# Relu and square of a finished block issued behind the next product's splits, and the two-block group put first in the first down step

## The chip, the cores and the metric

The kernel runs on one core of one Trainium2 chip. The metric is device time in microseconds (us) of one execution, and the time quoted is the median over runs.

## The reference, cut to what matters

One decoder layer: a normalised input feeds three head groups (stick-breaking attention, an SSD scan, an HGRN2 scan), their outputs are projected back, and then comes the squared-ReLU MLP. The change lies wholly in that MLP.

```python
hn = rmsnorm(h, norm_mlp_w[l])
h = h + jnp.square(jax.nn.relu(hn @ w_up[l])) @ w_down[l]
return h[:, CHUNK:]
```

After the meta tokens are dropped there are 1024 tokens; w_up is 1024 x 4096 and w_down 4096 x 1024, all float32.

## The kernel before, in words

**Products.** Both MLP products are done by a Strassen-like scheme: seven products of sums of half-size blocks instead of eight of blocks. A float32 operand is split into a rounded high part and a remainder (`split`, line 1138: ScalarE casts the high part, VectorE subtracts it from the source), and a product is taken as high x high, high x low and low x high. So a product of the up projection (`product`, line 1175) is 12 matmuls of 128 x 512: four blocks of the contraction times three.

**Up projection.** w_up is taken in 16 groups q of two column blocks. Two of the seven products of each q (names L) run first. The other five form a *quad* and run in the order written out in `order_` (line 1509): S5(q), R7(q), R6(q+1), S3(q), R4(q), then S5(q+1) and so on. `right_mm` (line 1280) accumulates R6, R7 and R4 of one q in one PSUM bank (tag pa, two buffers) and S5 and S3 in another (tag pc, two buffers). Behind each product but S5 stands a drain on VectorE (`right_post`, line 1288): R6's sum goes to `ra`; R7's drain is two additions, from the pa bank and then from the pc bank, and makes block u22; S3's drain makes u12, R4's makes u21. S3 accumulates in the same pc bank that R7's second addition reads, so S3's first matmul has to wait for it. Each of u22, u12 and u21 then gets Relu and Square on ScalarE (`square`, line 1257); u22 and u12 are also stored to DRAM (`dr_s[6]`, `dr_s[3]`).

**Sums of the blocks.** The next projection needs sums of the four squared blocks u22, u11, u12, u21. `u_sums(q, 0)` (line 1264) makes two on VectorE, `u_sums(q, 1)` two on GpSimd, each with a store through SyncE's queue. They are issued one and two items behind R4(q). Other work on GpSimd: four subtractions for a later q's weights (`sum_1`, `sum_2`, `sum_4`), the second of them the input of that q's R6 (`t2s`).

**Down projection.** It runs in 17 steps of seven products. `STEPS` (line 1311) lists for each step pairs (t, ks): t is one of four token blocks, ks the blocks of the contraction, 3 matmuls each. Step 0 holds t=1 with one block and t=2 with two, 9 matmuls in each product. Each (step, t) has its own accumulating bank; the first two banks of tag pa in step 0 are those that the last two quads leave. The weights of this projection are split by `t_aux` (line 1366; the hidden activations by `s_aux`, line 1387), which also makes sums (GpSimd for the first 14, VectorE after); the first `t_aux` is issued 24 items before the down projection begins, at D0.

**What sets the order.** The main loop (line 1558) goes through `order_`. For each item i it issues, in this order: the split of item i+2 (`prep`), the side jobs listed for i (`at`: loads, sums, `t_aux`, `s_aux`), the matmuls of i, and the drain of i. VectorE, ScalarE, GpSimd and SyncE work through what was issued to them strictly in that order (`Pinned`), and TensorE takes the products in the order of `order_`. Split tiles have the tag k4 and four buffers.

Of the kernel before, what the change touches and what calls it, by code (L numbers as in the profile page):

```python
# [68 lines left out]
def tile_hybrid_block(  # L69
# [34 lines left out]
    V, A, G, SY = (Pinned(e) for e in (nc.vector, nc.scalar, nc.gpsimd, nc.sync))  # L104
# [28 lines left out]
    def sb(shape, tag, dt=F32):  # L133
        if tag in ring:
            r = ring[tag]
            r[3] += 1
            at = r[0] + r[3] % r[1] * r[2]
            return cx[:, at:at + shape[0]]
        cnt[0] += 1
        return pool.tile([P] + list(shape), dt, tag=tag, bufs=BUFS[tag], name=f"{tag}_{cnt[0]}")  # L140
# [8 lines left out]
    def dram(shape, name):  # L149
        return drp.tile(list(shape), F32, name=name)  # L150
# [13 lines left out]
    dr_s = [dram([NQ, P, 512], f"dr_s{i}") for i in range(7)]  # L164
# [27 lines left out]
    def run(steps):  # L192
        for _ in steps:
            pass
# [1006 lines left out]
    def left_mm(q, h):  # L1201
        if h == 0:
            banks[q] = ps(("mf", "pb", "mf", "mq")[q % 4])
        yield from product(banks[q], lw[q, h], [hn[a][:, 4 * h:4 * h + 4] for a in range(2)], start=h == 0)

    def left_post(q, h):
        if h == 0:
            t = sb([512], ("a1", "a3")[q % 2])
            A.copy(t, banks[q])
            SY.dma_start(dr_m[q], t)  # L1210
        else:
            t = sb([512], ("a4", "sst")[q % 2])
            A.activation(t, banks[q], AF.Relu)
            A.activation(t, t, AF.Square)
            SY.dma_start(dr_s[0][q], t)
# [37 lines left out]
    def c_tile(q, i):  # L1253
        us[q, i] = sb([512], (("a4", "st", "st", "st"), ("qb", "sst", "a2", "f4"))[q % 2][i])
        return us[q, i]

    def square(c):
        A.activation(c, c, AF.Relu)
        A.activation(c, c, AF.Square)

    def u11_load(q):
        SY.dma_start(c_tile(q, 1), dr_s[0][q])
# [17 lines left out]
    def right_mm(o, q):  # L1280
        if o == "R6":
            Rb[q] = ps("pa")
        elif o == "S5":
            Sb[q] = ps("pc")
        yield from product(Sb[q] if o[0] == "S" else Rb[q], rw[o, q],
                           S[{"R6": "s2", "S5": "s1", "R7": "s3", "S3": "s4", "R4": "22"}[o]], start=o in ("R6", "S5"))

    def right_post(o, q):
        if o == "R6":
            ra[q] = sb([512], ("igt", "f4")[q % 2])  # L1290
            V.tensor_tensor(ra[q], Rb[q], m1s[q], op=ALU.add)
        elif o == "R7":
            c = c_tile(q, 0)
            V.tensor_tensor(c, Rb[q], m1s[q], op=ALU.add)
            V.tensor_tensor(c, Sb[q], c, op=ALU.add)
            square(c)
            SY.dma_start(dr_s[6][q], c)
        elif o == "S3":
            c = c_tile(q, 2)
            V.tensor_tensor(c, Sb[q], ra[q], op=ALU.add)  # L1300
            square(c)
            SY.dma_start(dr_s[3][q], c)
        elif o == "R4":
            c = c_tile(q, 3)
            V.tensor_tensor(c, Rb[q], m1s[q], op=ALU.add)
            square(c)

    STEPS = [[(1, [0]), (2, [0, 1])], [(3, [0, 1, 2])]]
    STEPS += [[(s % 4, list(range(s, s + 4)))] for s in range(13)]
    STEPS += [[(1, [13, 14, 15])], [(2, [14, 15]), (3, [15])]]
    acc, Tu, Su, Tr, Sr, slabs = {}, {}, {}, {}, {}, []
# [18 lines left out]
    def s_unit(o):  # L1333
        if o not in Su:
            if o < 4:
                t = sb([K4], "k4", F32R)[:, 0:D].rearrange("p (a k n) -> p a k n", a=2, n=P)
                Su[o] = [t[:, 0], t[:, 1]]
            else:
                Su[o] = [sb([512], t, F32R).rearrange("p (k n) -> p k n", n=P)
                         for t in (("st", "st"), ("a1", "a3"), ("a4", "st"))[o - 4]]  # L1340
        return Su[o]
# [9 lines left out]
    def s_load(m):  # L1351

        s, o = divmod(m, 7)
        if s >= len(STEPS):
            return
        Sr[m] = sb([512], ("wT", "wT", "a5", "igt")[m % 4]).rearrange("p (k n) -> p k n", n=P)
        n = 0
        for t, ks in STEPS[s]:
            src = dr_s[o][ks[0]:ks[-1] + 1, :, t * P:(t + 1) * P]
# [27 lines left out]
    def s_aux(m):  # L1387
        s, o = divmod(m, 7)
        n = sum(len(ks) for _, ks in STEPS[s])
        u = s_unit(o)  # L1390
# [24 lines left out]
    def down_mm(s, o):  # L1415
        n = 0
        for t, ks in STEPS[s]:
            c = CHAIN[o][0]
            key = (t, c) if c == "T" else (s, t, c)
            start = key not in down_banks  # L1420
            if start:
                down_banks[key] = ps({"R": "pa", "S": "pc", "T": M2B[t]}[c])
            pd = down_banks[key]
            ops = [(i, a, b) for i in range(len(ks)) for a, b in ((0, 0), (0, 1), (1, 0))]
            for m, (i, a, b) in enumerate(ops):
                mm(pd, lhsT=Su[o][a][:, n + i, :], rhs=t_unit(o, ks[i])[:, b, :], start=start and m == 0,
                   stop=m == len(ops) - 1, skip_group_check=not start)
                yield
            n += len(ks)

    def down_post(s, o):
        c, i, j = CHAIN[o]
        for t, ks in STEPS[s]:
            end = ks[-1] == NQ - 1
            if c == "T" and not end:
                continue
            r = t + 4 * i
            if r not in acc:
                acc[r] = sb([G3], "g3")[:, 0:D]
            rs, cs = place(t, i, j)  # L1440
            dst = acc[r][:, cs]
            bank = down_banks[(t, c) if c == "T" else (s, t, c)]
            if (r, j) in begun:
                V.tensor_tensor(dst, bank, dst, op=ALU.add)
            else:
                A.copy(dst, bank)
                begun.add((r, j))
            if end and o >= 3:
                SY.dma_start(outf[rs, cs], dst)
# [72 lines left out]
    def when(i, fn, *args):  # L1522
        at.setdefault(max(0, i), []).append((fn, args))

    for q in range(NQ):
        i6, i7, i4 = (order_.index((o, q)) for o in ("R6", "R7", "R4"))
        when(i6 - 8, quad_load, q)
        when(i6 - 4, sum_1, q)
        when(i6 - 3, sum_2, q)
        when(i6 - 2, m1_load, q)  # L1530
        when(i4 + 1, u_sums, q, 0)
        when(i4 + 2, u_sums, q, 1)
        when(i7, u11_load, q)
    for b in ("11", "12", "22", "21"):
        when(D0 - 28, t_load, b, 0)
# [11 lines left out]
    def prep(i):  # L1547
        if i < D0:
            it = order_[i]
            if it[0] == "L":  # L1550
                if i:
                    left_prep(it[2], it[1])
            else:
                right_prep(*it)
# [3 lines left out]
    for i, it in enumerate(order_):  # L1558
        if i + 2 < len(order_):
            prep(i + 2)  # L1560
        for fn, args in at.get(i, ()):
            fn(*args)
        if it[0] == "L":
            run(left_mm(it[2], it[1]))
            left_post(it[2], it[1])
            next(bg, None)
        elif it[0] == "D":
            run(down_mm(it[1], it[2]))
            down_post(it[1], it[2])
        else:  # L1570
            run(right_mm(*it))
            right_post(*it)
# [23 lines left out]
```

## Time and profile before

| | |
|---|---|
| median of 3 runs | 1271.08 us (1270.58 to 1273.02) |
| the profiled execution's own time | 1271.42 us |
| its span | 1269.4 us |
| TensorE matmul busy | 1215.4 us, 96% of the span |
| VectorE busy | 868.9 us, 68% |
| ScalarE busy | 582.8 us, 46% |
| GpSimd busy | 426.9 us, 34% |
| quads (R6 of q=0 to the last R4) | 719 to 951 us after the span's start |
| down projection | 951 to 1263 us |

In the views, PE is TensorE, PEld its weight loads, DVE VectorE, ACT ScalarE, POOL GpSimd and SPq the queue of SyncE that issues DMAs. A row of a timeline gives the start, the duration, engine, line and operation, out<-in (tags without buffer numbers and without digits: k is k4, a is a1 to a5), and in brackets the idle time in front of it with what ended that. Nearly everything has line 96 or 119, since two helpers record the instructions; tiles tell them apart. A matmul's row ends later than the next one starts, because matmuls are pipelined: 12 in a row start over 2.72 us.

### The profile page before, as it was taken

How to read it: one execution, taken by the hardware profiler on the slowest of the kernel's cores; microseconds unless marked ns; L12 is line 12 of the kernel's file. 1: busy time of each engine (PE TensorE's matmuls, PEld its weight loads, DVE VectorE, ACT ScalarE, POOL GpSimd, SP SyncE). 2: the span in 40 equal slices, each digit the busy share in tenths (PEclk: the TensorE clock that was granted, in tenths of full speed). 3: DMA queues.
4: the chain of work that ended last, by engine and by line, in shares of the span. 5: the costliest groups of instructions: out<-in, count | busy, mean ns of one | idle time of the engine just before them, and what ended most of it. 6: DMA issues, size and time to landing. Idle time of an engine off the chain costs nothing.

```text
span 1269.4 us, 18555 instructions
## 1 busy us (share of the span) xinstructions
PE 1215.4 (96%) x6362; PEld 1037.4 (82%) x6362; DVE 868.9 (68%) x1449; ACT 582.8 (46%) x1237; POOL 426.9 (34%) x500
## 2 busy tenths in 40 slices
PE   7999999999999889998999999999797999999998
PEld 6989899999888777777788887777576888888887
DVE  5777777774325688787356665566667787787777
ACT  6755666664322323322366544444455544344331
POOL 4223223322103476667342656566731000000000
PEclk9999999999999899999999999999998999999999
DMA  6311111242335754561256666767656645545556
GB/s 205 93 40 45 57 43 49 70 126 81 94 103 140 231 155 111 121 134 39 83 183 192 214 205 211 232 226 249 213 173 199 179 143 150 166 142 149 165 188 207
DMA packets 195031, 184.14 MB, mean 145 GB/s; under 512 B 14405, under 2 KB 149853, under 8 KB 194938
## 3 DMA queue, kind: packets, MB, share of 16 engines
q1 hardware_dynamic: 194938, 182.97, 48.2%
q8 instruction: 50, 0.82, 0.3%
q14 instruction: 43, 0.35, 0.1%
HBM read 128.25 MB, written 54.67 MB: 144 GB/s over the span
## 4 chain that ended last, share of the span: by engine, by line
PE 64%; DVE 15%; ACT 8%; issue 6%; DMA 4%; POOL 3%; SPq 0%; ACTq 0%; DVEq 0%; POOLq 0%
PE mf L119 23%; PE pa L119 17%; PE pc L119 11%; PE mq L119 7%; DVE k L96 5%; PE pb L119 3%; ACT k L96 3%; DVE g L96 2%; DVE a L96 2%; DVE qb L96 1%; ACT a L96 1%; PE pb L122 1%; POOL cx L96 1%; DVE st L96 1%; PE pa L122 1%
## 5 line engine op out<-in xcount | busy, mean ns | idle before, releaser
L119 PE MATMUL pa<-g,k 128*128 128x512 f32 x864 | 211.2, 392 | 8.3 <-DVE f L96 6.7
L119 PEld LDWEIGHTS pa<-g,k 128*128 128x128 f32 x864 | 162.4, 189 | 44.3 <-DVE f L96 7.2
L119 PE MATMUL mf<-g,wsA 128*128 128x384 f32 (+2 forms) x624 | 139.3, 358 | 0.0
L119 PE MATMUL mf<-g,wsB 128*128 128x384 f32 (+2 forms) x624 | 136.5, 355 | 0.0
L96 DVE TENSOR_TENSOR k<-g,k 128x512 fp32r<-128x512 f32 x80 | 74.9, 937 | 69.6 <-ACT k L96 69.6
L119 PEld LDWEIGHTS mf<-g,wsA 128*128 128x128 f32 x624 | 104.4, 190 | 6.5 <-DVE wsA L96 0.3
L119 PEld LDWEIGHTS mf<-g,wsB 128*128 128x128 f32 x624 | 103.6, 189 | 6.1
L119 PE MATMUL mf<-g,g 128*128 128x512 f32 (+1 forms) x408 | 100.8, 394 | 0.0
L96 ACT CAST g<-cx 128x512 fp32r<-128x512 f32 x80 | 49.6, 620 | 83.5 <-DVE cx L96 59.9
L119 PEld LDWEIGHTS mf<-g,g 128*128 128x128 f32 (+1 forms) x408 | 72.4, 183 | 15.1 <-issue 0.3
L119 PE MATMUL pc<-g,k 128*128 128x512 f32 x336 | 83.2, 391 | 0.0
L96 DVE TENSOR_TENSOR g<-pa,g 128x512 f32<-128x512 f32 (+2 forms) x82 | 54.9, 678 | 38.4 <-PE pa L119 32.2
L96 POOL TENSOR_TENSOR cx<-cx 128x384 f32<-128x384 f32 (+2 forms) x34 | 39.0, 1147 | 120.4 <-ACT cx L96 78.5
L119 PEld LDWEIGHTS pc<-g,k 128*128 128x128 f32 x336 | 63.7, 190 | 13.4
L119 PE MATMUL mf<-g,k 128*128 128x512 f32 x288 | 69.6, 392 | 1.8 <-ACT a L96 1.5
L119 PE MATMUL pa<-g,st 128*128 128x512 f32 x240 | 65.0, 389 | 0.0
L119 PEld LDWEIGHTS mf<-g,k 128*128 128x128 f32 x288 | 53.6, 188 | 13.6 <-ACT a L96 1.9
L96 POOL TENSOR_TENSOR g<-g,g 128x512 f32<-128x512 f32 x32 | 46.3, 1454 | 49.7 <-issue 45.5
L96 DVE TENSOR_TENSOR g<-cx,g 128x512 fp32r<-128x512 f32 x80 | 57.0, 712 | 7.0 <-ACT g L96 5.6
L96 ACT CAST k<-g 128x512 fp32r<-128x512 f32 x80 | 48.9, 613 | 15.6 <-PE pb L119 11.4
L96 DVE TENSOR_TENSOR k<-wT,k 128x512 fp32r<-128x512 f32 (+1 forms) x56 | 40.7, 726 | 18.7 <-ACT k L96 18.7
L119 PEld LDWEIGHTS pa<-g,st 128*128 128x128 f32 x240 | 45.0, 188 | 9.6 <-ACT g L96 0.2
(358 smaller groups left out, 2713.7 us busy)
## 6 DMA issues: line engine op xcount, KB each, us to landing
g<-in_w_up_dram SPq DMA_DIRECT2D x48, 512.0 KB, 4.8
st<-in_w_in_dram SPq DMA_DIRECT2D x51, 256.0 KB, 2.9
cx<-in_w_down_dram SPq DMA_DIRECT2D x48, 256.0 KB, 2.9
wT<-dr_s SPq DMA_DIRECT2D x45, 256.0 KB, 2.9
dr_s<-a SPq DMA_DIRECT2D x40, 256.0 KB, 2.0
g<-in_x_dram SPq DMA_DIRECT2D x16, 512.0 KB, 5.3
dr_s<-st SPq DMA_DIRECT2D x32, 256.0 KB, 2.2
a<-dr_s SPq DMA_DIRECT2D x23, 256.0 KB, 2.9
```

The lines of the kernel that those rows point to most:

```text
L96: i = fn(*a, **k)
L119: return queue(nc.tensor.matmul(*a, **k))
L122: return queue(nc.tensor.transpose(*a, **k))
```

## The change

`square` no longer follows the drain at once. `right_post` puts the finished block (and its store, if it has one) on a list `late`; the main loop takes it from there in the next item, after that item's split and side jobs and before its matmuls. The two `u_sums` of a q are issued one item later than before. In step 0 of the down projection the group t=2 with two blocks now comes before t=1 with one.

```diff
--- before.py
+++ after.py
@@ -1254,9 +1254,13 @@
         us[q, i] = sb([512], (("a4", "st", "st", "st"), ("qb", "sst", "a2", "f4"))[q % 2][i])
         return us[q, i]
 
-    def square(c):
+    late = []
+
+    def square(c, dst=None):
         A.activation(c, c, AF.Relu)
         A.activation(c, c, AF.Square)
+        if dst is not None:
+            SY.dma_start(dst, c)
 
     def u11_load(q):
         SY.dma_start(c_tile(q, 1), dr_s[0][q])
@@ -1293,22 +1297,20 @@
             c = c_tile(q, 0)
             V.tensor_tensor(c, Rb[q], m1s[q], op=ALU.add)
             V.tensor_tensor(c, Sb[q], c, op=ALU.add)
-            square(c)
-            SY.dma_start(dr_s[6][q], c)
+            late.append((c, dr_s[6][q]))
         elif o == "S3":
             c = c_tile(q, 2)
             V.tensor_tensor(c, Sb[q], ra[q], op=ALU.add)
-            square(c)
-            SY.dma_start(dr_s[3][q], c)
+            late.append((c, dr_s[3][q]))
         elif o == "R4":
             c = c_tile(q, 3)
             V.tensor_tensor(c, Rb[q], m1s[q], op=ALU.add)
-            square(c)
-
-
-
-
-    STEPS = [[(1, [0]), (2, [0, 1])], [(3, [0, 1, 2])]]
+            late.append((c,))
+
+
+
+
+    STEPS = [[(2, [0, 1]), (1, [0])], [(3, [0, 1, 2])]]
     STEPS += [[(s % 4, list(range(s, s + 4)))] for s in range(13)]
     STEPS += [[(1, [13, 14, 15])], [(2, [14, 15]), (3, [15])]]
     acc, Tu, Su, Tr, Sr, slabs = {}, {}, {}, {}, {}, []
@@ -1528,8 +1530,8 @@
         when(i6 - 4, sum_1, q)
         when(i6 - 3, sum_2, q)
         when(i6 - 2, m1_load, q)
-        when(i4 + 1, u_sums, q, 0)
-        when(i4 + 2, u_sums, q, 1)
+        when(i4 + 2, u_sums, q, 0)
+        when(i4 + 3, u_sums, q, 1)
         when(i7, u11_load, q)
     for b in ("11", "12", "22", "21"):
         when(D0 - 28, t_load, b, 0)
@@ -1560,6 +1562,8 @@
             prep(i + 2)
         for fn, args in at.get(i, ()):
             fn(*args)
+        while late:
+            square(*late.pop(0))
         if it[0] == "L":
             run(left_mm(it[2], it[1]))
             left_post(it[2], it[1])
```

On ScalarE, in a quad in the middle (that from 757 us on in the trace), there stood before, from the Square of S3's block on (k4_1083 is R7's high part, st_1087 R4's block, k4_1088 the high part for R6, k4_1091 that for S3, qb R7's block, k4_1094 that for R4):

```order
L96 ACTIVATE st_1082_7399<-st_1082_7399 128x512 x2
L96 CAST k4_1083_7404<-g3_1051_7178 128x512
L96 ACTIVATE st_1087_7426<-st_1087_7426 128x512 x2
L96 CAST k4_1088_7430<-wT_1084_7407 128x512
L96 CAST k4_1091_7453<-g3_1052_7180 128x512
L96 ACTIVATE qb_1093_7474<-qb_1093_7474 128x512 x2
L96 CAST k4_1094_7480<-g3_1052_7180 128x512
```

On ScalarE at the same place there stands now:

```order
L96 CAST k4_1083_7401<-g3_1051_7175 128x512
L96 ACTIVATE st_1082_7399<-st_1082_7399 128x512 x2
L96 CAST k4_1088_7428<-wT_1084_7404 128x512
L96 ACTIVATE st_1087_7426<-st_1087_7426 128x512 x2
L96 CAST k4_1091_7449<-g3_1052_7177 128x512
L96 CAST k4_1094_7473<-g3_1052_7177 128x512
L96 ACTIVATE qb_1093_7470<-qb_1093_7470 128x512 x2
```

Each pair of Relu and Square (`ACTIVATE ... x2`) has moved behind one cast: R7's high part no longer stands behind S3's Square, nor R6's behind R4's, nor R4's behind R7's.

On VectorE in the same quad, from the low part for R7 on (st_1087<-pa is R4's drain, the two rows with only st and a4 are `u_sums`, the two qb rows R7's drain), before:

```order
L96 TENSOR_TENSOR k4_1083_7404<-g3_1051_7178,k4_1083_7404 128x512
L96 TENSOR_TENSOR st_1087_7426<-pa_1061_7251,a1_1055_7206 128x512
L96 TENSOR_TENSOR k4_1088_7430<-wT_1084_7407,k4_1088_7430 128x512
L96 TENSOR_TENSOR a4_1076_7358<-st_1087_7426,a4_1076_7358 128x512
L96 TENSOR_TENSOR st_1087_7426<-st_1075_7344,st_1087_7426 128x512
L96 TENSOR_TENSOR k4_1091_7453<-g3_1052_7180,k4_1091_7453 128x512
L96 TENSOR_TENSOR qb_1093_7474<-pa_1078_7367,a3_1072_7322 128x512
L96 TENSOR_TENSOR qb_1093_7474<-pc_1090_7440,qb_1093_7474 128x512
L96 TENSOR_TENSOR k4_1094_7480<-g3_1052_7180,k4_1094_7480 128x512
```

On VectorE at the same place there stands now:

```order
L96 TENSOR_TENSOR k4_1083_7401<-g3_1051_7175,k4_1083_7401 128x512
L96 TENSOR_TENSOR st_1087_7426<-pa_1061_7251,a1_1055_7200 128x512
L96 TENSOR_TENSOR k4_1088_7428<-wT_1084_7404,k4_1088_7428 128x512
L96 TENSOR_TENSOR k4_1091_7449<-g3_1052_7177,k4_1091_7449 128x512
L96 TENSOR_TENSOR a4_1076_7354<-st_1087_7426,a4_1076_7354 128x512
L96 TENSOR_TENSOR st_1087_7426<-st_1075_7340,st_1087_7426 128x512
L96 TENSOR_TENSOR qb_1093_7470<-pa_1078_7367,a3_1072_7316 128x512
L96 TENSOR_TENSOR qb_1093_7470<-pc_1090_7436,qb_1093_7470 128x512
L96 TENSOR_TENSOR k4_1094_7473<-g3_1052_7177,k4_1094_7473 128x512
```

The two sums have moved behind the low part for S3 (k4_1091); they still stand ahead of R7's drain.

On VectorE where the up projection ends (st_1299<-pa is R4's drain of q=14, a2<-pc S3's of q=15, f4<-pa R4's of q=15, which is the last product; g1 rows are `t_aux`, the 128x384 rows `s_aux` of step 0), before:

```order
L96 TENSOR_TENSOR st_1299_8907<-pa_1267_8671,a1_1261_8620 128x512
L96 TENSOR_TENSOR a4_1280_8777<-st_1299_8907,a4_1280_8777 128x512
L96 TENSOR_TENSOR st_1299_8907<-st_1279_8763,st_1299_8907 128x512
L96 TENSOR_TENSOR g1_1300_8915<-kto_62,g1_1300_8915 128x512
L96 TENSOR_TENSOR k4_1301_8919<-wT_1283_8789,k4_1301_8919 128x384
L96 TENSOR_TENSOR a2_1303_8937<-pc_1292_8843,f4_1287_8811 128x512
L96 TENSOR_TENSOR g1_1300_8915<-cx_61,g1_1300_8915 128x512
L96 TENSOR_TENSOR k4_1304_8949<-a5_1284_8792,k4_1304_8949 128x384
L96 TENSOR_TENSOR f4_1306_8967<-pa_1286_8798,a3_1276_8741 128x512
L96 TENSOR_TENSOR qb_1295_8877<-f4_1306_8967,qb_1295_8877 128x512
L96 TENSOR_TENSOR f4_1306_8967<-sst_1294_8859,f4_1306_8967 128x512
```

On VectorE at the same place there stands now:

```order
L96 TENSOR_TENSOR st_1299_8907<-pa_1267_8671,a1_1261_8614 128x512
L96 TENSOR_TENSOR g1_1300_8909<-kto_62,g1_1300_8909 128x512
L96 TENSOR_TENSOR k4_1301_8913<-wT_1283_8786,k4_1301_8913 128x384
L96 TENSOR_TENSOR a2_1303_8933<-pc_1292_8843,f4_1287_8811 128x512
L96 TENSOR_TENSOR a4_1280_8773<-st_1299_8907,a4_1280_8773 128x512
L96 TENSOR_TENSOR st_1299_8907<-st_1279_8759,st_1299_8907 128x512
L96 TENSOR_TENSOR g1_1300_8909<-cx_61,g1_1300_8909 128x512
L96 TENSOR_TENSOR k4_1304_8942<-a5_1284_8789,k4_1304_8942 128x384
L96 TENSOR_TENSOR f4_1306_8963<-pa_1286_8798,a3_1276_8735 128x512
L96 TENSOR_TENSOR g1_1300_8909<-cx_61,g1_1300_8909 128x512
L96 TENSOR_TENSOR cx_61<-cx_61 128x512
```

The sums of q=14 have moved from ahead of S3's drain to behind it, and those of q=15 from right behind the last drain to behind three more operations of the down projection.

## The prediction

> **What bounds the kernel now.** I read the busy table and the page's 40 slices first (TensorE is busy 96% of the span and at full clock nearly throughout), then what TensorE waits for in the stretch that the change touches, then the timelines of TensorE, VectorE and ScalarE around the longest waits. TensorE's waits from the first quad to the second down step (microseconds in total, times, longest):
>
> ```profile
> PE pa L119 <- DVE f L96: 6.7, 1, 6.7
> PE pc L119 <- DVE qb L96: 4.0, 4, 2.5
> PE pc L119 <- DVE a L96: 3.7, 3, 2.5
> PE pa L119 <- ACT k L96: 1.5, 1, 1.5
> ```
>
> The pc rows are S3 waiting for R7's drain; the pa row with f is the down projection waiting for the bank that the last R4 leaves. The table by stretch counts short waits too: nine quads (from S3 to S3), the next four, the rest of the last quads up to R7(15)'s end, R4(14) to the wait's end, down step 0, and the rest of the down projection (length, then busy time of PE, PEld, DVE, ACT, POOL, then the granted clock).
>
> ```profile
> 743.46:869.71 126.25, 124.80 (x542) 100.67 (x541) 75.01 (x108) 57.36 (x100) 77.51 (x55) 1.00 0.68 225
> 869.71:934.31 64.60, 56.73 (x240) 44.24 (x241) 41.85 (x56) 29.65 (x53) 41.26 (x30) 1.00 0.66 212
> 934.31:942.58 8.27, 8.27 (x37) 6.84 (x38) 4.66 (x8) 6.05 (x11) 3.62 (x3) 1.00 0.81 253
> 942.58:958.31 15.73, 9.00 (x40) 7.13 (x38) 10.51 (x16) 7.10 (x14) 4.40 (x3) 0.92 0.59 192
> 958.31:974.67 16.36, 16.05 (x60) 12.64 (x61) 14.55 (x22) 11.57 (x23) 3.30 (x2) 0.87 0.65 196
> 974.67:1263.30 288.63, 288.63 (x1274) 238.83 (x1273) 230.53 (x366) 114.91 (x209) 0.00 (x0) 1.00 0.55 165
> ```
>
> What these lengths would be without waits follows from a quad's rows, R4, S5, then R7 with R6 of the next q, then S3:
>
> ```profile
> 760.18 2.88 PE L119 MATMUL pa<-g,k 128*128 128x512 f32 x12
> 762.90 2.88 PE L119 MATMUL pc<-g,k 128*128 128x512 f32 x12
> 765.62 5.60 PE L119 MATMUL pa<-g,k 128*128 128x512 f32 x24
> 771.68 0.47 PE L119 MATMUL pc<-wsA,k 128*128 128x512 f32 x1 [0.46 <-DVE qb L96]
> ```
>
> A product of 12 matmuls takes 762.90 - 760.18 = 2.72, so a quad takes 13.60 and nine matmuls of a down product 2.04. S3 could have started at 765.62 + 5.44 = 771.06 and started 0.62 later. Lost time: 126.25 - 9 x 13.60 = 3.85 in nine quads; 64.60 - 4 x 13.60 = 10.20 in the next four; 8.27 - 3 x 2.72 = 0.11; and 32.09 - (3 x 2.72 + 7 x 2.04 = 22.44) = 9.65 from R4(14) through step 0. Together 23.81. Behind 974.67 PE is busy 288.63 of 288.63 at clock 1.00, so what is won ahead of it moves the end by as much, and nothing is left to win there.
>
> **Why R7's drain is late.** The same quad on ScalarE and VectorE (st is R4's block, the first k the high part of R6, a<-st the first of `u_sums`, qb R7's drain):
>
> ```profile
> 765.75 1.30 ACT L96 ACTIVATE st<-st 128x512 f32<-128x512 f32 x2 [1.36 <-DVE st L96]
> 766.95 0.60 ACT L96 CAST k<-wT 128x512 fp32r<-128x512 f32 x1
> ```
>
> ```profile
> 765.03 0.68 DVE L96 TENSOR_TENSOR st<-pa,a 128x512 f32<-128x512 f32 x1
> 767.59 0.69 DVE L96 TENSOR_TENSOR k<-wT,k 128x512 fp32r<-128x512 f32 x1 [1.87 <-ACT k L96]
> 768.20 0.69 DVE L96 TENSOR_TENSOR a<-st,a 128x512 f32<-128x512 f32 x1
> 768.92 0.69 DVE L96 TENSOR_TENSOR st<-st,st 128x512 f32<-128x512 f32 x1
> 769.53 0.69 DVE L96 TENSOR_TENSOR k<-g,k 128x512 fp32r<-128x512 f32 x1
> 770.13 0.68 DVE L96 TENSOR_TENSOR qb<-pa,a 128x512 f32<-128x512 f32 x1
> 770.85 0.69 DVE L96 TENSOR_TENSOR qb<-pc,qb 128x512 f32<-128x512 f32 x1
> ```
>
> R4's drain ends at 765.71, the pair of Relu and Square runs to 767.05, the cast behind it to 767.55, and VectorE, 1.87 idle, takes up the low part at 767.59. Two sums and a low part later it reaches R7's drain at 770.13, though R7 had ended at 768.34. The drain ends at 771.54, and S3 starts.
>
> **Quads: what the change does.** It adds and removes no operation: three pairs of 1.30, five casts and the 12 VectorE operations of a quad stay. It takes the pair out of the path drain, pair, cast, low part. I follow one quad by these durations, from R4's end at 762.90 (a row runs on 0.16 past the pitch: 763.06). The drain runs to 763.75; the low part of R6, whose cast is done ahead, to 764.4; the pair on ScalarE to 765.05, the cast for S3 to 765.6; low part to 766.3, two sums to 767.7. R7 ends at 768.34 + 0.16, its drain runs from 768.5 to 769.9, and S3's turn is at 771.06. The wait is gone with 1.16 to spare, and VectorE was idle 0.8 ahead of the drain: about 2 of slack. Next in line is the next split, which has two products of time.
>
> GpSimd can still hold VectorE up:
>
> ```profile
> 892.66 1.78 DVE L96 TENSOR_TENSOR g<-cx,g 128x512 fp32r<-128x512 f32 x1
> ```
>
> ```profile
> 892.08 1.81 POOL L96 TENSOR_TENSOR g<-g,g 128x512 f32<-128x512 f32 x1
> ...
> 748.94 1.30 POOL L96 TENSOR_TENSOR g<-g,g 128x512 f32<-128x512 f32 x1
> 750.19 1.75 POOL L96 TENSOR_TENSOR g<-g,wT 128x512 f32<-128x512 f32 x1
> ```
>
> An operation of 0.69 takes 1.78 where one of GpSimd runs (892.08 to 893.89), and GpSimd's 1.30 becomes 1.81 where VectorE was first: they take turns. Drains that read PSUM stay at 0.68. In turns, a GpSimd operation takes 1.25 (748.94 to 750.19) and one of VectorE on SBUF alone 0.60 (769.53 to 770.13). Of VectorE's 108 operations in the nine quads 45 are drains: 55 x 1.25 + 63 x 0.60 = 106.6 of 122.4. That fits, and the whole 3.85 goes. In the next four quads, where `t_aux` comes in, 30 x 1.25 + 36 x 0.60 (56 less 20 drains) = 59.1 of 54.4: 4.7 too much, of which one GpSimd operation (1.25) can hang over the end. So 3.5 to 4.7 stays where the turns are taken without gaps; I take 4.0 of 10.20. Bounds: 0 where the overhang fits into idle time before and after, 10.20 as today.
>
> The Trainium skill ("SBUF — State Buffer", section on the two separate sides) says that GpSimd and VectorE share a pair of ports under an exclusive lock, and that a VectorE operation with two SBUF inputs is blocked for a whole GpSimd instruction. The rows above agree. By that rule at its worst, each GpSimd operation holding VectorE up in full, the late quads would take 56 x 0.60 + 30 x 1.25 = 71.1 of 54.4 and lose 16.7 instead of my 4.0; the trace shows 41.85 - 33.6 = 8.2 of such blocking, not 37.5.
>
> **The end of the up projection.**
>
> ```profile
> 939.86 5.60 PE L119 MATMUL pa<-g,k 128*128 128x512 f32 x24
> 948.01 3.56 PE L119 MATMUL pa<-g,k 128*128 128x512 f32 x15
> 958.31 2.93 PE L119 MATMUL pa<-g,k 128*128 128x512 f32 x6 [6.74 <-DVE f L96]
> 961.04 2.90 PE L119 MATMUL pc<-g,k 128*128 128x512 f32 x9
> 963.78 0.40 PE L119 MATMUL pa<-g,k 128*128 128x512 f32 x1
> ```
>
> ```profile
> 950.48 0.69 DVE L96 TENSOR_TENSOR a<-st,a 128x512 f32<-128x512 f32 x1 [1.36 <-ACT st L96]
> ...
> 952.41 1.62 DVE L96 TENSOR_TENSOR k<-wT,k 128x384 fp32r<-128x384 f32 x1
> 953.95 0.68 DVE L96 TENSOR_TENSOR a<-pc,f 128x512 f32<-128x512 f32 x1
> 956.50 0.69 DVE L96 TENSOR_TENSOR g<-cx,g 128x512 fp32r<-128x512 f32 x1 [1.86 <-ACT g L96]
> ...
> 957.57 0.68 DVE L96 TENSOR_TENSOR f<-pa,a 128x512 f32<-128x512 f32 x1
> ```
>
> The last R4 ends at 948.01 + 2.72 = 950.73; three matmuls of group t=1 follow, then 6.74 of waiting for the last drain (957.57 to 958.25). VectorE had waited 1.36 for a Square and 1.86 for a cast behind one, and been held up about 1.05 by GpSimd (1.62 for an operation of 0.55). Behind the wait six matmuls take 2.73 instead of 1.36 and nine 2.74 instead of 2.04: 2.07 for a lower clock, and the table has 0.87 for step 0. The waits of up to 2.5 in the quads left it at 1.00.
>
> Now, with T for the last R4's end: S3(15)'s drain starts at T - 2.55 and no Square stands ahead of it. Behind it come two sums, a low part of `t_aux`, one of `s_aux`, then the last drain. Six at 0.60 to 0.72 and one hold-up of 1.05 to 1.30 put its end at about T + 2.4. Group t=2, now first, fills TensorE to T + 1.36 (six matmuls; three gave 0.68 before), so about 1.1 of waiting is left of 6.74, and no clock is lost. If the hold-up stays away, nothing is left.
>
> Then step 0. VectorE has the same work in less time. From S3(15)'s drain to the drain of product 4, which product 6 waits for, stand 23 operations: 23 x 0.60 = 13.8, and four of GpSimd (the sums of q=14 and 15) hold it up by 1.05 each: 18.0, from T - 2.55 to T + 15.45. TensorE without waits would want product 6 at T + 6 x 2.04 = T + 12.24. So 3.2 stays, the 1.1 included; 0 if nothing is held up (T + 11.25), 6.4 if it also waits for ScalarE as at 950.48 and 956.50 (1.36 + 1.86). Step 1's first bank is now the one with six matmuls, filled 0.68 before its turn and copied in 0.6: nothing.
>
> **Other queues.** On SyncE's queue the stores of u22 and u12 now stand behind the next weight load, and those of the sums behind the load of m1; no reader of them is near. One could bite: f4, stored by `u_sums`, is written again by R6's drain of q+2.
>
> ```profile
> dr_s<-st SPq DMA_DIRECT2D x32, 256.0 KB, 2.2
> ```
>
> It lands 2.2 after issue. The sums end at about 0.6 before R7's end, that drain starts 2.72 after it: 1.1 to spare. I price it at nothing, and at up to 1 in a late quad.
>
> **Sum.** Left over are 0 + 4.0 + 3.2 = 7.2 of 23.8, so 16.6 is won: 1271.42 (the profiled execution) - 16.6 = 1254.8. That execution lies 0.34 above the median of the runs, so I say 1254.5. Own range: 1251 to 1258.5.
>
> **Rivals.**
> (a) All waits go, since VectorE's and GpSimd's turns fall into idle time. For it: VectorE is busy only 41.85 of 64.60 in the four late quads. Against it: the 59.1 above. 0.5 is left: 1247.8.
> (b) The turns bind as hard as the Squares did: the late quads lose 10.2 as today and step 0 loses 6.4. 16.6 is left, 7.2 won: 1263.9. For it: GpSimd is busy 41.26 of 64.60 there. By the rule of the Trainium skill quoted above ("SBUF — State Buffer"), blocking for whole instructions, half of the 16.7 would be enough for the late quads' part. To (b) I count that the sums, still ahead of R7's drain and still behind R4's Square, keep S3 late although the order changed.
> (c) Slower: R6's cast now stands ahead of R4's pair. Its input is made by GpSimd:
>
> ```profile
> 747.67 1.31 POOL L96 TENSOR_TENSOR wT<-g,wT 128x512 f32<-128x512 f32 x1 [1.88 <-issue]
> 737.90 5.60 PE L119 MATMUL pa<-g,k 128*128 128x512 f32 x24
> ```
>
> It is there at 748.98, 8.4 after R7's end (740.62). R4's drain ends 9.0 after R7's end (three products, 0.16 and 0.68), so the cast delays nothing today. Where the input came over 0.6 + 2 later, pair, sums and R7's drain would all wait for it, in each quad. With 2 us for each of 13 quads, 26 + 3.2 are lost instead of 23.8: 1276.5. That takes it at 13 instead of 8.4. Against it: GpSimd's sums start earlier with the change, since the sums on VectorE end at 767.7 in the walk above and at 769.6 today (768.92 + 0.69).
> (d) What is won in the quads is waited for again in the late quads and step 0: no change, 1271.1. For it speaks nothing that I see, against it that VectorE idles today in both.
>
> **Chances.** Forecast 0.58, (a) 0.14, (b) 0.20, (c) 0.05, (d) 0.03. A measurement of this kernel can tell about 0.2%, 2.5 us, from no change. Faster 0.92, same 0.03, slower 0.05. The range 1248 to 1262.5 holds the forecast, most of (a) and the better part of (b).
>
> **What would show it.** S3 following R6 at once in the nine quads (VectorE idle ahead of R7's drain, no 1.87 in front of a low part); four late quads of 54.4 + 4; the 6.74 down to about 1; clock 1.00 in step 0; a wait of products 4 to 6 of step 0 for VectorE. Wrong would be: S3 still late in the steady quads, ScalarE waiting for GpSimd ahead of R6's cast, or waits behind 975.

## The result, and the profile after

The changed kernel takes 1251.6 us (median of 4 runs, 1251.18 to 1251.74), the kernel before 1271.42 beside it (4 runs, 1270.58 to 1273.02): a ratio of 0.9842, 95% interval 0.9825 to 0.9859. The forecast was 1254.5. The profiled execution has a span of 1249.5 instead of 1269.4. Its busy times, to be set against the table of before:

```profile
PE 1209.6 (97%) x6362; PEld 1037.4 (83%) x6362; DVE 885.8 (71%) x1449; ACT 584.0 (47%) x1237; POOL 429.9 (34%) x500
```

What TensorE waits for between the first quad and the second down step (us in total, times, longest):

```profile
PE pa L119 <- DVE g L96: 0.9, 1, 0.9
PE pa L119 <- DVE f L96: 0.8, 1, 0.8
PE pc L119 <- DVE a L96: 0.6, 1, 0.6
```

The 6.7 is gone, of the longer waits of S3 for R7's drain one of 0.6 is left, and the longest of all, product 6 of step 0 waiting for VectorE, is 0.9 (the seven products of a step are counted from 0). Four stretches of the table, cut as before: nine steady quads from S3 to S3, the four late quads, R7(15)'s end to down step 1, and the steps behind step 1 (length, busy PE, PEld, DVE, ACT, POOL, granted clock):

```profile
743.04:865.45 122.41, 122.41 (x542) 101.35 (x541) 80.73 (x108) 58.26 (x100) 77.99 (x55) 1.00 0.70 232
865.45:921.16 55.71, 54.99 (x241) 44.73 (x240) 50.14 (x56) 28.98 (x52) 41.99 (x29) 1.00 0.71 236
...
929.40:954.90 25.50, 23.50 (x100) 18.16 (x98) 24.40 (x36) 17.84 (x35) 7.73 (x5) 1.00 0.76 238
...
969.48:1243.30 273.82, 273.82 (x1210) 226.81 (x1209) 218.99 (x348) 106.50 (x193) 0.00 (x0) 1.00 0.55 165
```

The nine quads take 122.41 where 122.40 is the time without waits: 0.01 lost instead of 3.85. The four late ones take 55.71: 1.31 lost instead of 10.20. From R7(15)'s end to step 1 it is 25.50 - 22.44 = 3.06 instead of 9.65, with a clock of 1.00 instead of 0.92 and 0.87. Behind that PE is busy all the time, as it was.

One steady quad of the changed kernel, on TensorE (R7 with R6, then S3), ScalarE (R4's pair, the cast for S3) and VectorE (R4's drain, low part of R6, low part of S3, the second of the two sums, R7's drain):

```profile
764.80 5.60 PE L119 MATMUL pa<-g,k 128*128 128x512 f32 x24
770.25 0.39 PE L119 MATMUL pc<-wsA,k 128*128 128x512 f32 x1
```

```profile
763.01 1.30 ACT L96 ACTIVATE st<-st 128x512 f32<-128x512 f32 x2 [0.91 <-DVE st L96]
764.21 0.60 ACT L96 CAST k<-g 128x512 fp32r<-128x512 f32 x1
```

```profile
762.28 0.69 DVE L96 TENSOR_TENSOR st<-pa,a 128x512 f32<-128x512 f32 x1 [1.05 <-PE pa L119]
762.89 0.68 DVE L96 TENSOR_TENSOR k<-wT,k 128x512 fp32r<-128x512 f32 x1
764.85 0.69 DVE L96 TENSOR_TENSOR k<-g,k 128x512 fp32r<-128x512 f32 x1 [1.27 <-ACT k L96]
...
766.18 0.69 DVE L96 TENSOR_TENSOR st<-st,st 128x512 f32<-128x512 f32 x1
767.73 0.69 DVE L96 TENSOR_TENSOR qb<-pa,a 128x512 f32<-128x512 f32 x1 [0.85 <-PE pa L119]
```

S3 starts 5.45 after R7, at once. R4's pair still stands ahead of a cast and a low part still waits 1.27 for it, but the two sums are through at 766.87, and VectorE then idles 0.85 until R7 ends.

The end of the up projection, on TensorE and VectorE (18 matmuls are the last R4 and six of group t=2; f<-pa is the last drain):

```profile
934.85 4.24 PE L119 MATMUL pa<-g,k 128*128 128x512 f32 x18
939.89 0.98 PE L119 MATMUL pa<-g,k 128*128 128x512 f32 x3 [0.81 <-DVE f L96]
...
952.61 0.70 PE L119 MATMUL pa<-g,a 128*128 128x512 f32 x2 [0.88 <-DVE g L96]
```

```profile
939.16 0.68 DVE L96 TENSOR_TENSOR f<-pa,a 128x512 f32<-128x512 f32 x1
...
944.08 1.67 DVE L96 TENSOR_TENSOR cx<-kto,cx 128x512 f32<-128x512 f32 x1
945.66 1.65 DVE L96 TENSOR_TENSOR st<-wT,st 128x384 fp32r<-128x384 f32 x1
```

The last R4 ends at 934.85 + 2.72 = 937.57, its drain at 939.84, and 0.81 of waiting is left of 6.74. The last two rows take 1.67 and 1.65 instead of 0.69 and 0.55: there GpSimd makes the sums of q=15. Product 6 of step 0 waits 0.88 for VectorE.

### The profile page after: what moved, and what is told of

The parts are those of the page before. It is cut to its first block, busy times and chain, and to the rows that moved or that the text cites. A ratio compares the mean times of both kernels' runs of the same rounds, so it can differ in the third digit from the quotient of the medians.

```text
span 1249.5 us, 18592 instructions
## 1 busy us (share of the span) xinstructions
PE 1209.6 (97%) x6362; PEld 1037.4 (83%) x6362; DVE 885.8 (71%) x1449; ACT 584.0 (47%) x1237; POOL 429.9 (34%) x500
## 4 chain that ended last, share of the span: by engine, by line
PE 78%; DVE 9%; POOL 3%; ACT 3%; issue 3%; DMA 3%; SPq 0%; POOLq 0%; ACTq 0%; DVEq 0%
PE pa L119 25%; PE mf L119 23%; PE pc L119 17%; PE mq L119 7%; PE pb L119 3%; DVE k L96 3%; DVE g L96 2%; PE pb L122 1%; POOL cx L96 1%; DVE a L96 1%; PE pa L122 1%; DVE cx L96 1%; DVE wT L96 1%; PE pc L122 1%; ACT g L96 1%
## 5 line engine op out<-in xcount | busy, mean ns | idle before, releaser
L96 DVE TENSOR_TENSOR k<-g,k 128x512 fp32r<-128x512 f32 x80 | 81.0, 1013 | 28.6 <-ACT k L96 28.0
L96 DVE TENSOR_TENSOR g<-cx,g 128x512 fp32r<-128x512 f32 x80 | 60.5, 756 | 4.9 <-ACT g L96 3.5
L96 DVE SCALAR_TENSOR_TENSOR cx<-cx,cwb 128x384 f32<-128x384 f32 (+1 forms) x72 | 43.5, 605 | 9.2 <-ACT cx L96 8.6
```

Source lines behind the costliest of these rows:

```text
L96: i = fn(*a, **k)
```

## The experiments

Executions differ in what comes ahead of the quads: the second S3 starts anywhere from 742.68 to 746.21 us, though nearly all the code ahead of it is the same, and the changed kernel itself reached it at 743.04 once and at 746.21 another time. So I compare what lies behind it. *Behind* is the span less the start of the second S3; the losses are lengths less the time without waits (122.40 for nine quads, 54.40 for the four late ones, 44.88 from the S3 of q=14 to step 2, six products of 2.72 and two down steps of seven products of 2.04).

| run | time | second S3 | behind | nine quads | late quads | end |
|---|---|---|---|---|---|---|
| before | 1271.42 | 743.46 | 525.94 | 3.85 | 10.20 | 9.90 |
| after | 1251.60 | 743.04 | 506.46 | 0.01 | 1.31 | 3.44 |
| 1 Squares ahead of side jobs, sums at old places | 1258.55 | 743.67 | 513.03 | 0.00 | 2.23 | 8.84 |
| 2 groups in the old order | 1251.94 | 744.01 | 505.69 | 0.00 | 1.02 | 3.00 |
| 3 before, sums later | 1274.27 | 744.50 | 527.70 | 5.77 | 10.41 | 9.84 |
| 4 before, groups in the new order | 1272.96 | 744.93 | 526.07 | 3.75 | 10.18 | 10.15 |
| 5 only R4's pair behind | 1262.65 | 744.63 | 516.07 | 0.07 | 7.28 | 7.04 |
| 6 all but R4's pair behind | 1257.87 | 743.91 | 511.99 | 0.00 | 3.61 | 6.62 |
| 7 last sums ten items later | 1254.34 | 742.68 | 509.52 | 0.00 | 1.31 | 6.43 |
| 8 the same, on VectorE | 1250.91 | 743.81 | 505.39 | 0.00 | 1.31 | 2.35 |
| 9 sums of `t_aux` on VectorE | 1255.65 | 743.68 | 510.12 | 0.00 | 4.94 | 3.49 |
| 10 last sums far off, on VectorE | 1250.46 | 744.84 | 503.76 | 0.00 | 1.33 | 0.71 |
| 11 the same, one `t_aux` moved | 1249.85 | 742.90 | 503.70 | 0.00 | 1.28 | 0.74 |
| 12 after, again | 1253.83 | 746.21 | 506.49 | 0.00 | 1.32 | 3.40 |

Runs 1 to 10 are one execution each; beside runs 1 to 8 the kernel before took 1274.77, beside 9 and 10 1271.72. Runs 11 and 12 are medians of 4 on one chip, where the kernel before took 1271.82. Each of the other columns is read from one profiled execution. Behind the second S3 the two of the changed kernel agree within 0.03; but the late quads of run 2, whose code there is the same, lose 1.02 and theirs 1.31 and 1.32, so a few tenths between two runs say nothing.

**Which part of the change does it: runs 3, 4 and 2.** The theory was that only the moved Relu and Square pairs count. Run 3 is the kernel before with the sums one item later:

```diff
-        when(i4 + 1, u_sums, q, 0)
-        when(i4 + 2, u_sums, q, 1)
+        when(i4 + 2, u_sums, q, 0)
+        when(i4 + 3, u_sums, q, 1)
```

> The kernel before with nothing but the sums issued one item later; Relu and Square stay at the drain. Theory: R7's drain is as late as before (walked through with the old rows: 770.2 instead of 770.13 in the quad shown), quads lose 13 to 15 us as before, the last wait shrinks from 6.7 to about 6: 1270 to 1272 us. Rival (the sums' place carries the gain): 1258 to 1262 us.

Its time is above the theory's 1270 to 1272, and behind the second S3 it is 1.76 slower than before. In this one execution the later sums without the later pairs win nothing and lose a little, and the last wait shrank only to 6.57, where about 6 was expected; VectorE waits 27 times and 50.6 us for ScalarE in the nine quads, as it did before.

Run 4 is the kernel before with the new first step:

```diff
-    STEPS = [[(1, [0]), (2, [0, 1])], [(3, [0, 1, 2])]]
+    STEPS = [[(2, [0, 1]), (1, [0])], [(3, [0, 1, 2])]]
```

> The kernel before with nothing but the two-block group first in down step 0. Theory: the wait of 6.7 becomes 6.1 and the clock still drops behind it: 1270.4 to 1271.4 us. Rival (the group order matters more than its 0.68, as by saving the clock): 1268 to 1269 us.

The time (1272.96) is above both, but the run reached the second S3 1.47 later than that of before, and behind it takes 526.07 against 525.94: nothing won. The first wait of the down projection fell from 6.74 to 6.05, as it should, and most of it was lost again by a lower clock behind the wait (12 matmuls in 5.28 us, which take 2.72 at full speed: 2.56 lost there, against 2.07 in the kernel before). Run 2 is the changed kernel with the old first step (the same lines the other way round):

> The changed kernel with the one-block group first again in down step 0. Theory (step 0 is bound by VectorE's list of 23 operations): the first wait grows by 0.68 to about 1.5 us, the later waits of step 0 shrink by nearly as much, the time from R7(15)'s end to step 1's first matmul stays 25.5 within 0.3: 1251.6 to 1251.9 us. Rival (the two-block group hides 0.68 of a real wait): 26.2 and 1252.3 us.

```profile
940.47 1.65 PE L119 MATMUL pa<-g,k 128*128 128x512 f32 x6 [1.47 <-DVE f L96]
...
953.18 0.70 PE L119 MATMUL pa<-g,a 128*128 128x512 f32 x2 [0.83 <-DVE g L96]
```

The wait at the last drain is 1.47 instead of 0.81, as expected; but product 6 waits 0.83 as with the new order, and the end loses 3.00 instead of 3.44. Product 6 starts 15.03 behind the last R4's end (938.15), with the new order 15.04: what the new order saves at the first wait is spent again before product 6. The time lies 0.04 above the theory's range (1251.94), and from R7(15)'s end at 929.99 to step 1 at 955.30 it is 25.3, within it: the new order of the groups moves 0.66 of waiting from one place to another and wins nothing.

**Which pair: runs 5 and 6.** Run 5 moves only R4's pair and leaves the others at their drains:

```diff
-            late.append((c, dr_s[6][q]))
+            square(c, dr_s[6][q])
...
-            late.append((c, dr_s[3][q]))
+            square(c, dr_s[3][q])
```

> The changed kernel with only R4's pair of Relu and Square deferred; those of R7 and S3 stay at the drain. Theory (every pair holds up the next low part on VectorE, and either link broken is enough in a steady quad): steady quads lose 0 to 1 us in all, the late quads about 5, the first down product waits about 1.7: 1255 to 1259 us. Rival (R4's pair ahead of R6's cast is the whole cause): quads without loss, 1251 to 1253 us.

Run 6 leaves R4's pair at its drain and moves the others:

```diff
-            late.append((c,))
+            square(c)
```

> The changed kernel with R7's and S3's pairs deferred and R4's at the drain, ahead of R6's cast. Theory: R4's drain itself comes early since S3's pair no longer holds up the low part ahead of it; steady quads lose 0, the late quads 1 to 4: 1251.5 to 1255 us. Rival (R4's pair is the whole cause): quads lose 10 to 14, 1262 to 1266 us.

Both times lie above the theory's ranges, run 5 by 3.65 and run 6 by 2.87, and neither lies in the rival's: moving only some of the pairs leaves more than I held. (In run 6 the quads are as expected, 0.00 and 3.61 lost; its excess is at the end.) The nine quads and VectorE's waits in them, in run 5:

```profile
744.63:867.10 122.47, 122.47 (x541) 101.26 (x540) 79.96 (x108) 57.04 (x100) 73.74 (x55) 1.00 0.69 232
```

```profile
DVE k L96 <- ACT k L96: 42.1, 27, 1.9
```

and run 6:

```profile
743.91:866.31 122.40, 122.40 (x542) 101.38 (x540) 86.68 (x109) 57.41 (x100) 78.09 (x55) 1.00 0.70 232
```

```profile
DVE k L96 <- ACT k L96: 16.8, 9, 1.9
```

In the nine quads either suffices, R4's pair alone or the other two together: 0.07 and 0.00 are lost. Neither R7's pair nor S3's was moved alone. In the late quads R7's and S3's pairs together count for more than R4's, 3.61 left in run 6 against 7.28 in run 5; at the end both leave most of the loss, 6.62 and 7.04. The same waits in the kernel before and in the changed one, in that order:

```profile
DVE k L96 <- ACT k L96: 50.6, 27, 1.9
```

```profile
DVE k L96 <- ACT k L96: 11.5, 9, 1.3
```

Before, VectorE was busy 75.01 and waited 50.6 for ScalarE, 125.6 of 126.25, and it waited for nothing else: 27 waits of 1.87, three in each quad, one for each pair. Its round of a quad was longer than TensorE's, and that set the pace. In run 5 it still waits 27 times, 42.1 in all, and 79.96 + 42.1 fills 122.1 of 122.47: just enough, with no slack. In run 6 it is nine waits and 16.8.

**Behind the split or behind the side jobs: run 1.** In the changed kernel, the pairs are issued behind the split but ahead of the side jobs, and the sums at their old places:

```diff
+        while late:
+            square(*late.pop(0))
         for fn, args in at.get(i, ()):
             fn(*args)
-        while late:
-            square(*late.pop(0))
...
-        when(i4 + 2, u_sums, q, 0)
-        when(i4 + 3, u_sums, q, 1)
+        when(i4 + 1, u_sums, q, 0)
+        when(i4 + 2, u_sums, q, 1)
```

> The changed kernel with the pairs of Relu and Square issued behind the split but ahead of the side jobs of the next item, and the sums at their old places (one and two items behind R4). Theory (what counts in the quads is that a pair no longer stands ahead of the next split's cast): the nine steady quads stay at 13.60 each, the late quads lose 1 to 4 us, and at the end of the up projection, where the sums of q=14 and a pair stand ahead of the last drain again, the first down product waits about 3.7 us instead of 0.8: 1254 to 1258 us. Rival (the later place of the sums carries the gain): the quads lose their 14 us again, 1265 to 1271 us.

It took 1258.55, half a us above the theory and far from the rival. The quads are won (0.00 and 2.23), the end is not: 8.84. On VectorE (the first sum, a low part of `t_aux`, the last drain) and TensorE there:

```profile
937.49 0.69 DVE L96 TENSOR_TENSOR a<-st,a 128x512 f32<-128x512 f32 x1 [1.36 <-ACT st L96]
...
943.54 0.69 DVE L96 TENSOR_TENSOR g<-cx,g 128x512 fp32r<-128x512 f32 x1 [1.86 <-ACT g L96]
...
944.61 0.68 DVE L96 TENSOR_TENSOR f<-pa,a 128x512 f32<-128x512 f32 x1
```

```profile
936.31 4.24 PE L119 MATMUL pa<-g,k 128*128 128x512 f32 x18
```

The last R4 ends at 939.03, and its drain begins 5.58 later instead of 1.59: the sums stand ahead of it again and wait 1.36 for a Square, and a cast of `t_aux` stands behind another pair (1.86). So at the end it matters that the pairs stand behind the side jobs' casts too, or that the sums come later, or both; run 1 does not part these two.

**What is left at the end: runs 7, 8 and 10.** Run 7 puts the sums of the last q (they are not read before the last down steps) ten and eleven items later:

```diff
-        when(i4 + 2, u_sums, q, 0)
-        when(i4 + 3, u_sums, q, 1)
+        when(i4 + 2 + 10 * (q == NQ - 1), u_sums, q, 0)
+        when(i4 + 3 + 11 * (q == NQ - 1), u_sums, q, 1)
```

> The changed kernel with the sums of q=15 put off into down step 1 (items 11 and 13 of the down projection), where VectorE idles. Theory (the drain that product 6 of step 0 waits for stands behind a list of 23 VectorE operations and four hold-ups by GpSimd): two operations and two hold-ups leave the list, 3.4 us; the waits of products 4 and 6 (0.3 and 0.9) go, the first wait of 0.8 stays, step 0 ends about 2 us sooner: 1249.4 to 1250.4 us. Rival (step 0 waits for something else, a DMA or ScalarE): within 0.5 of 1251.6 us.

A miss: 1254.34, 3.06 us more behind the second S3 than the changed kernel. Step 0 did win (from the S3 of q=14 to step 1 it loses 1.36 instead of 3.14), but step 1 lost 5.07. On GpSimd, VectorE and TensorE:

```profile
963.73 1.66 POOL L96 TENSOR_TENSOR sst<-qb,sst 128x512 f32<-128x512 f32 x1 [23.71 <-DVE f L96]
965.47 1.60 POOL L96 TENSOR_TENSOR a<-a,sst 128x512 f32<-128x512 f32 x1
```

```profile
964.17 1.78 DVE L96 TENSOR_TENSOR cx<-kto,cx 128x512 f32<-128x512 f32 x1
965.87 1.75 DVE L96 TENSOR_TENSOR k<-a,k 128x512 fp32r<-128x512 f32 x1
```

```profile
968.37 1.19 PE L119 MATMUL pa<-g,a 128*128 128x512 f32 x2 [3.06 <-DVE g L96]
```

GpSimd's two sums now fall just ahead of VectorE's drain of product 4 of step 1 (at 967.55), hold VectorE up twice by 1.1, and product 6 waits 3.06; its nine matmuls then take 3.73 instead of 2.04. The hold-ups had only been moved. Run 8 gives these sums, and the second sums of q=14, to VectorE:

```diff
-            (V if n == 0 else G).tensor_tensor(dst, x, y, op=op)
+            (V if n == 0 or q >= NQ - 2 else G).tensor_tensor(dst, x, y, op=op)
```

> As the kernel with the sums of q=15 put off, and the second sums of q=14 and 15 on VectorE instead of GpSimd. Theory (one GpSimd operation blocks VectorE by about 1.1 us and costs more there than the 0.6 to 0.7 of doing it on VectorE): no stretched operation ahead of the last drain, the first wait goes from 0.8 to 0 to 0.6: 1248.8 to 1250 us. Rival (VectorE's own time counts, and GpSimd's help was worth it): 1 us slower than with GpSimd.

It missed its range of 1248.8 to 1250 by 0.91 (1250.91), of which 0.77 is the later start of the second S3 (743.81); 2.35 is lost at the end. The rival falls: behind the second S3 it is 4.13 faster than run 7, not slower. The last drain is in time; what is left is two waits for VectorE:

```profile
951.26 0.71 PE L119 MATMUL pa<-g,a 128*128 128x512 f32 x2 [0.48 <-DVE g L96]
...
966.99 0.70 PE L119 MATMUL pa<-g,a 128*128 128x512 f32 x2 [0.89 <-DVE g L96]
```

Run 10 is run 8 with the sums of the last q at `i4 + 2 + 29` and `i4 + 3 + 30`:

> The changed kernel with the sums of the last q put off by 29 and 30 items more, into the fourth down step or later, and the second sums of the last two q on VectorE. In the changed kernel 3.4 us are lost from the S3 of q=14 (921.16) to the start of down step 2 (969.48); with the sums put off by ten items and on VectorE it was 2.35 (921.92 to 969.15). Theory, that this loss is VectorE's load and GpSimd's hold-ups in steps 0 and 1: 0.3 to 1.2 is left, nothing is lost further back, time 1248.5 to 1250.0. Rival, that four operations of VectorE cost the same wherever they stand, since VectorE is busy 80% of the down projection: TensorE waits 1 to 2.5 where they now stand, time 1250.5 to 1252.

The end loses 0.71, PE is busy in all of it, and PE has no wait behind 970; the time of 1250.46 is half a us above the range, since the second S3 came 1.80 later than in the changed kernel (744.84):

```profile
922.97:968.56 45.59, 45.59 (x198) 36.96 (x199) 39.13 (x63) 32.65 (x62) 5.94 (x4) 1.00 0.68 206
```

So the loss at the end was VectorE's load in steps 0 and 1 and GpSimd's hold-ups there, not the work itself. How much each of the two is worth is not shown: no run put the sums this far off and left them to GpSimd.

**What is left in the late quads: runs 9 and 11.** Run 9 takes eight sums of `t_aux` from GpSimd to VectorE, five of them in the late quads:

```diff
-        E = G if k < 2 else V
+        E = V
```

> The changed kernel with the sums of t_aux for the first blocks on VectorE instead of GpSimd (eight operations, four or five of them in the four late quads). The changed kernel's four late quads (865.45 to 921.16) take 55.71 where 54.4 would be without loss. Theory that turns between GpSimd and VectorE on SBUF make that loss: some 24 GpSimd operations at 1.11 and 41 VectorE operations on SBUF alone at 0.60 give 51 of 54.4, so the late quads take at most 55.0 and the time is 1250.5 to 1251.3. Rival, that VectorE has simply too many operations there and is held up as much as before (50.14 busy, five more at 0.60, 2.2 of waits for ScalarE, 55.4 with nothing left for TensorE's own waits): the late quads take 56.5 to 58.5 and the time is 1252.5 to 1254.5.

The theory falls: it allowed 55.0. With 24 GpSimd operations instead of 29 the late quads take 59.34, more than either expected:

```profile
866.08:925.42 59.34, 56.45 (x242) 45.97 (x240) 49.14 (x61) 29.00 (x52) 34.15 (x24) 0.97 0.68 221
```

The place is one drain, R7's of q=12, with one of the moved sums right ahead of it on VectorE (cx) and held up by GpSimd:

```profile
892.78 1.65 DVE L96 TENSOR_TENSOR cx<-cx 128x512 f32<-128x512 f32 x1
894.36 0.68 DVE L96 TENSOR_TENSOR a<-pa,a 128x512 f32<-128x512 f32 x1
```

S3 waits 2.47 for it, and then loses 1.69 by a lower clock (its 12 matmuls run from 895.91 to 900.32, 4.41 instead of 2.72; more on this below). Without the 1.69 the late quads would have taken 57.65, inside the rival's 56.5 to 58.5, so run 9 does not speak against the rival. The same place in the changed kernel (qb<-f the first of `u_sums`, g<-cx the low part of the fourth `t_aux`, a<-pa the drain):

```profile
888.82 1.78 DVE L96 TENSOR_TENSOR qb<-f,qb 128x512 f32<-128x512 f32 x1
...
891.25 0.69 DVE L96 TENSOR_TENSOR g<-cx,g 128x512 fp32r<-128x512 f32 x1
891.85 0.69 DVE L96 TENSOR_TENSOR a<-pa,a 128x512 f32<-128x512 f32 x1
```

R7 had ended at 890.09 (it starts at 887.21, and runs 2.72 + 0.16). Run 11 is run 10 with that `t_aux` one item later:

```diff
-        when(D0 + (2 * j - 24 if j < 7 else -10 if j == 7 else j - 14 if j < 21 else j - 12), t_aux, j)
+        when(D0 + (2 * j - 24 + (j == 3) if j < 7 else -10 if j == 7 else j - 14 if j < 21 else j - 12), t_aux, j)
```

> The run before with the last sums put far off, and the fourth t_aux issued one item later, so that its low part no longer stands between u_sums and the drain of R7(12). In the changed kernel that drain started 1.76 after R7's end, of which 1.16 are to spare and 0.60 were waited for: 0.77 waiting for a cast, 1.10 held up by GpSimd, 0.60 for this low part. Theory, that what is lost in the late quads is such a local delay ahead of one drain: the wait of 0.60 goes, the four late quads take 54.9 to 55.2 instead of 55.7, and the time is 1248.9 to 1250.2, 1.5 to 2.7 below the changed kernel beside it. Rival, that the loss follows the number of VectorE's and GpSimd's operations in the stretch, which is the same: the late quads take 55.6 or more and the time is 1249.5 or more.

```profile
892.66 0.47 PE L119 MATMUL pc<-wsA,k 128*128 128x512 f32 x1
...
906.96 0.47 PE L119 MATMUL pc<-wsA,k 128*128 128x512 f32 x1 [0.45 <-DVE qb L96]
```

```profile
865.30:920.98 55.68, 55.08 (x242) 44.74 (x240) 50.70 (x56) 28.99 (x52) 41.96 (x29) 1.00 0.70 236
```

The wait of 0.60 is gone, and S3(13) has got one of 0.45 in its place. The late quads take 55.68, which is the rival's number: VectorE handed the delay on to the next quad. In the late quads it is busy 50.70 and waits 2.2 for ScalarE and 2.7 for TensorE, 55.6 of 55.68. What sets the 1.3, and which edit would take it away, stays open.

Run 12 is the changed kernel beside run 11:

> The changed kernel as it is, on the same chip as the run with all three further edits. 1251.2 to 1252.0 by every theory.

It took 1253.83 (1252.34 to 1254.71), above what was expected, and run 11 1249.85 (1248.51 to 1251.05). Behind the second S3 run 12 takes 506.49, where the first profile had 506.46; what differs lies ahead, and no run was made on that. So run 11 is 3.98 below run 12, where 1.5 to 2.7 were expected; between their profiled executions 3.31 lies ahead of the second S3 (742.90 and 746.21) and 2.79 behind it, nearly all of that at the end. Run 11 has the lowest time here: against before 0.9826 (0.9811 to 0.9841), against 0.9854 (0.9837 to 0.9870) of the changed kernel on that chip. Behind the second S3 it is level with run 10 (503.70 and 503.76): the moved `t_aux` won nothing that these runs show.

## Why the prediction was right, and where it was not

The mechanism held in the steady quads and at the end; in the late quads one term was too large, and that is most of what was off. The time of 1251.6 lies only 0.6 above the lower end of the forecast's own range, 1251.

- **Steady quads: right in size, too narrow in cause.** 3.85 was to go, 3.84 went, and VectorE idles 0.85 ahead of R7's drain where 0.8 was walked. But the prediction named one chain, R4's pair ahead of R6's cast. Run 6 leaves that very chain in place and loses nothing, and run 5 breaks only that chain and loses 0.07: VectorE's round was 0.4 a quad too long, and each of the three pairs held it up by 1.87.
- **Late quads: the mis-sized term.** The step was "30 x 1.25 + 36 x 0.60 ... = 59.1 of 54.4", of which 4.0 was to stay; 1.31 stayed, and this is nearly all of the 2.9 us by which the forecast was too high. GpSimd's turn adds 1.11 to VectorE's time, not 1.25, where the two engines alternate. On VectorE, two operations that are held up, and what follows them:

```profile
895.14 1.79 DVE L96 TENSOR_TENSOR k<-a,k 128x512 fp32r<-128x512 f32 x1
...
898.56 0.68 DVE L96 TENSOR_TENSOR st<-pc,igt 128x512 f32<-128x512 f32 x1
```

From 895.14 to 898.56 stand two such pairs of turns, 1.71 each, of which 0.60 are VectorE's. With the 29 that stand in this stretch now, instead of 30, the sum is 53.8 of 54.4. But run 9 shows that such a sum is no forecast either: it gives 51 for a stretch that took 59.34. There most of the loss came from what stands ahead of one drain and from the clock; run 11 cleared that place and the total stayed, so what sets the 1.31 is not shown. VectorE's waits for ScalarE in the late quads, before and after:

```profile
DVE k L96 <- ACT k L96: 22.5, 12, 1.9
```

```profile
DVE k L96 <- ACT k L96: 2.2, 4, 0.8
```

Of the 20.3 us that the change took from these waits, 8.3 came back as hold-ups by GpSimd (the same 56 operations of VectorE are busy 50.14 instead of 41.85).

- **End: right.** With T for the last R4's end: forecast 3.2, measured 3.06; the last drain was to end at T + 2.4 and ended at T + 2.27; the first wait was to be 1.1 and was 0.81; product 6 was to wait until T + 15.45 and started at T + 15.04; the clock stayed at 1.00. Credit for the order of the groups was misplaced: run 2 shows that the 0.68 is real at the first wait (0.66) and spent again before product 6 starts.
- **Nothing to win behind 975, and the store of f4:** as forecast. R6's drain waited for that store twice, 0.49 in the late quads and 0.27 just behind them, and TensorE does not wait right behind either.
- **Rivals.** (b), with turns as hard as the Squares, is out: 1.31 and not 10.2. (Half of the 16.7, which the prediction called enough for it, is only 8.4.) (a), no turns that bind, was 3.8 below the result, the forecast 2.9 above it. (c) and (d) are out: the nine quads lose 0.01, and late quads and end together 4.75 instead of 20.10, so nothing was slowed and what was won was not waited for again.

## What to carry to other kernels

When engine A waits a fixed time for engine B at every step of a round, add up A's busy time and these waits over one round and hold the sum against the round of the engine that should set the pace: here 14.0 against 13.6 a quad, so that moving one pair of the three (run 5), or the other two (run 6), was worth nearly the whole loss of the steady quads. Where less slack is left, look also at what is queued ahead of the one operation that is waited for: moving the last sums by ten items made the kernel slower while GpSimd made half of them (run 7), and faster with all of them on VectorE (run 8). And compare variants over the stretch that they share, since the time up to it varied by up to 3.5 us from run to run.

## What the runs showed of the hardware

**A wait of the same length sometimes costs TensorE its clock and sometimes does not.** S3 of q=12, its first matmul and the start of the next product, on TensorE, in the kernel before and then in run 4, whose code is the same up to there:

```profile
902.69 0.47 PE L119 MATMUL pc<-wsA,k 128*128 128x512 f32 x1 [2.47 <-DVE a L96]
...
905.53 2.88 PE L119 MATMUL pa<-g,k 128*128 128x512 f32 x12
```

```profile
904.05 0.77 PE L119 MATMUL pc<-wsA,k 128*128 128x512 f32 x1 [2.47 <-DVE a L96]
...
908.28 2.90 PE L119 MATMUL pa<-g,k 128*128 128x512 f32 x12
```

Behind the same 2.47 of waiting S3 takes 2.84 in the kernel before, at a granted clock of 1.00, and 4.23 in run 4, at 0.65; without a wait it is 2.72. So the first wait cost 0.12 more than it was long, the second 1.51. Runs 9 and 5 differ in the same way: 4.41 behind a wait of 2.47, 2.82 behind one of 2.50. The prediction's remark that waits of up to 2.5 leave the clock at 1.00 was true of one execution. The Trainium skill ("TensorE: Matmul & The Clock Gate", Part 1) says that the gate goes by a free-running window, and that the same kernel can come out differently from run to run; the kernel before and run 4 differ as it says. At what length of wait it begins, no run here shows: from the first quad on, the shortest that cost clock was 1.81 in run 6 (nine matmuls of step 0 then take 3.41 instead of 2.04, at 0.60), while one of 1.96 in run 1 cost 0.10.
